# Two 4 KB half buffers per block of expert weights, or one 8 KB buffer

## The chip, the cores and the metric

One core of one Trainium2 chip runs the whole kernel in one launch. The metric is the device time of a launch in microseconds (us); the kernel before took 1304.69 us (median of 3 runs, 1304.62 to 1304.88).

## The reference

A trunk of two layers over 256 tokens of width 1024, all in float32. Each layer has a mixer (three groups of heads that read one input projection, and one output projection) and then a mixture of 32 SwiGLU experts; each is followed by a residual and a layer norm. Cut to what matters here:

```
for i in range(DEPTH):                       # 2
    mix = hybrid_mixer(h, w_in[i], ..., w_out[i])
    h = layer_norm(ALPHA * h + mix)
    ffn = hierarchical_moe(h, ..., w_gate[i], w_up[i], w_down[i])
    h = layer_norm(ALPHA * h + ffn)
# one expert e:  (silu(xb @ w_gate[e]) * (xb @ w_up[e])) @ w_down[e]
# w_gate, w_up: (2, 32, 1024, 512), w_down: (2, 32, 512, 1024), float32
```

Every expert's weights are read once in each layer: 2 x 32 x 6 MB, 402.7 million bytes.

## The kernel before

**Experts.** A layer's experts are taken four at a time, in eight quarters (`for q in range(NE // QE)` in `moe`). The weights come in blocks of 1 MB: `blocks(l)` cuts each gate and up matrix into two blocks of 512 rows and each down matrix into two of 256 rows. The order is: first halves of four gates, second halves of four gates, the same for up, the same for down; 24 blocks a quarter, 192 a layer. In memory a block is 128 rows of 8 KB, one for each partition of the on-chip buffer. TensorE works on four blocks together (a group): `up` runs k outside and the four experts inside, so that a group starts in earnest when the last of its four blocks is there, and the four buffers are read to the end of the group. With `k` it goes through a block's four pieces of 512 columns in their order, so that the first 4 KB of each row are done with in the middle of a group.

**Buffers.** `load_rows(src, kind)` loads a block. Kind "R" takes one 8 KB buffer of the ring `w` (5 of them, `wslot`) with one DMA. Kind "H" takes two 4 KB buffers of the ring `wh` (10 of them, `whalf`) with a DMA of 512 KB each. In the steady part R and H alternate, so that of each group two blocks are R and two are H. Kind "X" is an 8 KB buffer of another ring (`wwide`), and a string such as "rrrr" is four 2 KB buffers (`wq`). The first 21 blocks of a layer have kinds written out by hand (`KINDS`, five of them H); they are issued while the mixer still runs, as buffers come free. The last five blocks before the final four of layer 1 are all H (`tail`), so that the R ring is free for the next layer's input weights. The last four blocks of a layer are loaded in 256 KB pieces (`load_last`, L1448). All of this goes through the queue of SyncE (SP) in one order; an issue that waits holds up those behind it.

**Split weights.** In the mixers the ring `wh` has another use: `split` makes of a weight piece a rounded high part (ScalarE, L404, listed under the helper's line L148) and the low rest (VectorE or GpSimd, L412), each in a 4 KB buffer, and `mm3` multiplies the parts in three matmuls for each k (L419, L420, L421). In the input projections L419 and L420 read the high part and L421 the low one. `ahead` keeps up to three splits ready.

Of the kernel before, what the change touches and what calls it, by code (L numbers as in the profile page):

```python
# [9 lines left out]
F32 = mybir.dt.float32  # L10
# [6 lines left out]
L, T, D = 2, 256, 1024  # L17
# [3 lines left out]
QE = 4  # L21
NR = 5
NX = 3
NH = 10
PB = dict(r=3, d=3, s=2)
WB = dict(x=1, r=27, d=9, s=7, sh=4)
PRI = ("r", "side", "s", "g", "d")
# [60 lines left out]
def hybrid_trunk(ctx, tc, x, w_in, w_sm, pp, sw, rows, w_r, lnv, cst, w_out,  # L88
# [3 lines left out]
    ring = ctx.enter_context(tc.tile_pool(name="ring", bufs=NR))  # L92
    hring = ctx.enter_context(tc.tile_pool(name="hring", bufs=NH))
    wk = ctx.enter_context(tc.tile_pool(name="wk", bufs=1))
# [3 lines left out]
    def shaped(t, shape):  # L98
        n = 1
        for s in shape:  # L100
            n *= s
        v = t[:, 0:n]
        if len(shape) == 2:
            v = v.rearrange("p (a b) -> p a b", a=shape[0])
        elif len(shape) == 3:
            v = v.rearrange("p (a b c) -> p a b c", a=shape[0], b=shape[1])
        elif len(shape) == 4:
            v = v.rearrange("p (a b c d) -> p a b c d", a=shape[0], b=shape[1], c=shape[2])
        return v
# [8 lines left out]
    def w512(*shape, name="w", tag=None):  # L118
        t = tag or cur[0]
        return shaped(wk.tile([128, 512], F32, tag="w_" + t, name=name, bufs=WB[t]), shape)  # L120
# [5 lines left out]
    def wide(name):  # L126
        return ring.tile([128, 2048], F32, tag="xs", name=name, bufs=NX)

    def quarters_of(v):
        return [[v[:, (2 * t + n) * 512:(2 * t + n + 1) * 512] for n in range(2)] for t in range(2)]  # L130
# [16 lines left out]
    def act(out, in_, func, **kw):  # L147
        i = nc.scalar.activation(out, in_, func, **kw)  # L148
        if func in tabs:
            chain_t(i)  # L150
        return i
# [4 lines left out]
    def after(a, b):  # L156

        tc.add_manual_dep(a.ins, b.ins.name, mybir.DependencyInfo(mybir.DependencyClass.NoSync,
                                                                  mybir.DependencyReason.DATA), reason="order")
# [234 lines left out]
    def slot():  # L394
        return ring.tile([128, 2048], F32, tag="w", name="wslot")
# [4 lines left out]
    def split(w, eng=None):  # L400

        n = w.shape[1:]
        hi = shaped(hring.tile([128, 1024], F32, tag="wh", name="whi"), n)
        i = act(hi.bitcast(F32R), w, AF.Copy)  # L404
        if last[0] is not None:
            after(i, last[0])
        last[0] = i
        nsub[0] += 1
        if eng is None:
            eng = G if nsub[0] % SUBV == 0 and nsub[0] > SV else V  # L410
        lo = shaped(hring.tile([128, 1024], F32, tag="wh", name="wlo"), n)
        i = eng.tensor_tensor(out=lo.bitcast(F32R), in0=w, in1=hi, op=OP.subtract)  # L412
        if eng is V and normed[0] is not None:
            after(i, normed[0])
        return hi.bitcast(F32R), lo.bitcast(F32R)
# [24 lines left out]
    def fetch(out, in_):  # L440

        i = nc.sync.dma_start(out=out, in_=in_)
        if order[0]:
            if order[0] is not True:
                after(i, order[0])
            order[0] = i

    def load_rows(src, kind):

        k, n = src.shape[0] // 128, src.shape[1]  # L450
        src = src.rearrange("(p k) c -> p (k c)", p=128)
        if kind in "RX":
            v = slot() if kind == "R" else wide("wwide")
            fetch(v, src)
            return [v[:, j * 512:(j + 1) * 512] for j in range(4)]
        if kind == "H":
            r = []
            for i in range(2):
                v = hring.tile([128, 1024], F32, tag="wh", name="whalf")
                fetch(v, src[:, i * 1024:(i + 1) * 1024])  # L460
                r += [v[:, 0:512], v[:, 512:1024]]
            return r
        r = []
        for j in range(4):
            v = w512(512, name="wq", tag=kind[j])
            fetch(v, src[:, j * 512:(j + 1) * 512])
            r.append(v)
        return r


    class Weights:
# [15 lines left out]
        def ahead(self, n, eng=None):  # L487

            while self.order and len(self.wp) < n:
                n_, m = self.order.pop(0)  # L490
                w = self.w[n_]
                self.wp[n_, m] = split(w[:, m] if isinstance(n_, int) else w[:, m * 4:(m + 1) * 4] if n_ == "gv"
                                       else w[:, :, m * 128:(m + 1) * 128], eng)
# [735 lines left out]
    def moe(l, src, part, early, WR, RT):  # L1229
# [79 lines left out]
        def residual(t, n):  # L1309

            p = ps(4, 128, tag="r" if t * 2 + n < RS0 else "s")
            for k in range(4):
                if 2 * t + n < RS0:
                    PE.transpose(p[:, k], h[t][n][:, k * 128:(k + 1) * 128], ident)
                    continue
                for a in range(2):
                    mm(p[:, k], lhsT=zp[a][t][n][:, k * 128:(k + 1) * 128], rhs=IDR.bitcast(F32R), start=(a == 0), stop=(a == 1))
            e = w512(4, 128, name="res", tag="s")
            for k in range(4):
                (A if 2 * t + n < RS0 else nc.scalar).activation(e[:, k], p[:, k], AF.Identity, scale=DP[:, l, 25 + 4 * n + k:26 + 4 * n + k],  # L1320
                    bias=DP[:, l, 33 + 4 * n + k:34 + 4 * n + k])
            yield
            for k in range(4):
                (PE.matmul if 2 * t + n < RS0 else mm)(acc[t][n][:, k * 128:(k + 1) * 128], lhsT=e[:, k], rhs=ident,
                                                       start=(k == 0 and 2 * t + n < RS0), stop=False)
# [93 lines left out]
        iota = c("iota", CAP)[:, None, :].to_broadcast([128, 2 * QE, CAP])  # L1419
        srcs = iter(blocks(l)[len(early):])  # L1420
        nb = 6 * NE - len(early) - QE
        tail = ["H"] * (NH // 2) if l + 1 < L else []
        kinds = iter(((["R", "H"] * nb)[:nb - len(tail)]) + tail)

        for i in range(ISSUE, len(early)):
            early[i] = load_rows(*early[i])
        order[0] = None

        def take():
            return early.pop(0) if early else load_rows(next(srcs), next(kinds))  # L1430
# [108 lines left out]
        for q in range(NE // QE):  # L1539
# [8 lines left out]
            r = residual(*divmod(q - RES + RS0, 2)) if 0 <= q - RES < 4 - RS0 else iter(())  # L1548
# [80 lines left out]
    src, h, gi, W = xin, xin, 0, Weights(0)  # L1629
# [5 lines left out]
    for l in range(L):  # L1635
        xT = transposed(src, h, p_(l, "gx", 0, 8), p_(l, "bx", 0, 8), between)
        if l == 0:
            setup()
        last[0] = last_x[LX]
        WR = w512(8, 36, name="WR", tag="x")  # L1640
        nc.sync.dma_start(out=WR, in_=w_r[l].rearrange("(k p) c -> p k c", p=128))
        F, part, RT = mixer(l, h, xT, gi, W, WR)
        if stages == "mixer":
            break
        early, order[0] = list(zip(blocks(l), KINDS)), True
        for i in range(ISSUE):
            early[i] = load_rows(*early[i])
        acc, zp, RM, GA, cnti = moe(l, F, part, early, WR, RT)
        overflow(l, zp, acc, RM, GA, cnti)
        if l + 1 < L:  # L1650
            W = Weights(l + 1)
            src, h, gi = acc, quarters_of(wide("h")), 4 + 4 * l
# [85 lines left out]
```

## Time and profile before

| | before |
|---|---|
| median of 3 runs | 1304.69 us |
| the profiled execution, its own time | 1305.92 us |
| its span in the trace | 1304.1 us |
| TensorE busy | 1038.0 us, 80% of the span |
| VectorE, ScalarE, GpSimd busy | 29%, 19%, 10% |
| read from memory | 440.82 MB |
| DMA packets | 127917, of them 104656 under 8 KB |

The span is the time from the first to the last instruction in the trace; the profiled execution's own time has 1.8 us around it. The busy shares are means over stages: two mixers (about 0 to 205 us and 650 to 845 us), and two stretches of experts behind them.

### The profile page before, as it was taken

Reading aid. Unit: us, or ns where it says so; the run is one execution under the profiler, and the core shown is the slowest. Engines: PE = TensorE matmul, PEld = TensorE weight load, DVE = VectorE, ACT = ScalarE, POOL = GpSimd, SP = SyncE. Lnnn points to the kernel's source line nnn. Section 1 sums busy time; section 2 is a strip of 40 time slices with the busy share of each in tenths; the row PEclk is TensorE's granted clock in tenths of the full one; section 3 lists DMA queues with packets and bytes.
Section 4 is the critical chain, followed back from the end, with each engine's and each line's share of the span. In section 5 each row is a group of like instructions: output and inputs, shape, how many; then the busy total and the mean of one; then the engine's idle time right before and its main releaser. Section 6 shows DMA issues by size and latency. Waiting matters only on the chain. (4 is left out here: it accounts for less than half of the span.)

```text
span 1304.1 us, 18012 instructions
## 1 busy us (share of the span) xinstructions
PE 1038.0 (80%) x7412; PEld 530.9 (41%) x7412; DVE 378.2 (29%) x842; ACT 252.1 (19%) x442; POOL 129.4 (10%) x121
## 2 busy tenths in 40 slices
PE   6899989787768677777788999896977777776765
PEld 5788783242123113211177887632411321131211
DVE  5888861020001000100269787510100110010002
ACT  4535532010000000000154453310100000010100
POOL 4234110000000000000033440100000000000001
PEclk9899989898998898898988999899889899889988
DMA  9343688999999999999973357699999999999995
GB/s 303 115 123 139 249 305 320 415 414 416 415 415 415 415 416 414 416 415 414 338 237 100 122 190 249 249 398 416 415 415 415 415 415 415 415 415 414 415 415 195
DMA packets 127917, 443.18 MB, mean 340 GB/s; under 512 B 16848, under 2 KB 41808, under 8 KB 104656
## 3 DMA queue, kind: packets, MB, share of 16 engines
q1 hardware_dynamic: 126256, 439.28, 86.3%
q10 hardware_dynamic: 1440, 2.62, 0.6%
q8 instruction: 62, 1.02, 0.3%
q14 instruction: 31, 0.25, 0.1%
q0 software_dynamic: 128, 0.01, 0.0%
HBM read 440.82 MB, written 1.05 MB: 339 GB/s over the span
## 5 line engine op out<-in xcount | busy, mean ns | idle before, releaser
L1489 PE MATMUL ps<-wslot,xg 128*32 128x512 f32 x968 | 323.1, 711 | 125.0 <-DMA wslot<-in_w_up_dram 88.1
L1489 PE MATMUL ps<-whalf,xg 128*32 128x512 f32 x984 | 317.7, 707 | 9.3 <-DMA whalf<-in_w_up_dram 7.9
L1489 PEld LDWEIGHTS ps<-wslot,xg 128*32 128x32 f32 x968 | 70.8, 126 | 345.4 <-issue 152.7
L1525 PE MATMUL ps<-wslot,hT 128*32 128x512 f32 x432 | 145.8, 631 | 26.8 <-DMA wslot<-in_w_down_dram 26.7
L1495 DVE TENSOR_TENSOR hh<-ps,hh 128x256 f32<-128x256 f32 x32 | 12.1, 419 | 495.6 <-PE ps L1489 429.6
L1525 PE MATMUL ps<-whalf,hT 128*32 128x512 f32 x448 | 148.1, 626 | 1.1 <-DMA whalf<-in_w_down_dram 1.1
L419 PE MATMUL ps<-xh,whi 128*128 128x256 f32 x320 | 95.7, 300 | 0.7 <-issue 0.7
L421 PE MATMUL ps<-xh,wlo 128*128 128x256 f32 x320 | 92.6, 290 | 2.7 <-DVE wlo L412 2.7
L420 PE MATMUL ps<-xl,whi 128*128 128x256 f32 x320 | 93.1, 292 | 0.0
L1489 PEld LDWEIGHTS ps<-whalf,xg 128*32 128x32 f32 x984 | 66.8, 125 | 56.4 <-DMA whalf<-in_w_up_dram 34.8
L1531 DVE SCALAR_TENSOR_TENSOR yy<-ps,gs,yy 128x512 fp32r<-128x512 f32 x32 | 24.0, 751 | 224.7 <-ACT yy L148 220.8
L412 POOL TENSOR_TENSOR wlo<-wslot,whi 128x1024 fp32r<-128x1024 f32 x26 | 63.3, 2436 | 143.5 <-ACT whi L148 113.3
L148 ACT ACTIVATE whi<-wslot 128x1024 fp32r<-128x1024 f32 x62 | 64.5, 1054 | 62.5 <-PE ps L420 48.7
L148 ACT ACTIVATE hT<-ps 128x256 f32<-128x256 f32 x32 | 12.3, 384 | 316.6 <-PE ps L1511 316.6
L1469 PE MATMUL ps<-oh,z 128*128 128x256 f32 x256 | 66.1, 418 | 7.8 <-DVE gs L1505 4.0
L1525 PEld LDWEIGHTS ps<-wslot,hT 128*32 128x32 f32 x432 | 30.9, 112 | 96.5 <-issue 50.0
L1469 PEld LDWEIGHTS ps<-oh,z 128*128 128x128 f32 x256 | 61.8, 329 | 16.2 <-issue 7.8
L148 ACT ACTIVATE yy<-ps,gs 128x512 fp32r<-128x512 f32 x32 | 22.0, 687 | 226.4 <-PE ps L1525 192.8
L421 PEld LDWEIGHTS ps<-xh,wlo 128*128 128x128 f32 x320 | 62.6, 196 | 4.1 <-DVE wlo L412 2.9
L419 PEld LDWEIGHTS ps<-xh,whi 128*128 128x128 f32 x320 | 62.6, 196 | 3.7 <-issue 2.0
L1534 PE MATMUL ps<-yy,gT 128*128 128x512 f32 x128 | 46.9, 447 | 21.3 <-ACT yy L148 16.0
L420 PEld LDWEIGHTS ps<-xl,whi 128*128 128x128 f32 x320 | 62.8, 197 | 2.0 <-issue 1.9
(386 smaller groups left out, 1251.5 us busy)
## 6 DMA issues: line engine op xcount, KB each, us to landing
whalf<-in_w_up_dram SPq DMA_DIRECT2D x134, 512.0 KB, 12.6
wslot<-in_w_gate_dram SPq DMA_DIRECT2D x62, 1024.0 KB, 13.8
wslot<-in_w_up_dram SPq DMA_DIRECT2D x59, 1024.0 KB, 13.8
whalf<-in_w_down_dram SPq DMA_DIRECT2D x112, 512.0 KB, 12.9
whalf<-in_w_gate_dram SPq DMA_DIRECT2D x112, 512.0 KB, 12.8
wslot<-in_w_down_dram SPq DMA_DIRECT2D x54, 1024.0 KB, 13.8
wslot<-in_w_in_dram SPq DMA_DIRECT2D x22, 1024.0 KB, 7.3
wq<-in_w_down_dram SPq DMA_DIRECT2D x64, 256.0 KB, 7.0
```

The costliest lines, as they stand in the source:

```text
L148: i = nc.scalar.activation(out, in_, func, **kw)
L412: i = eng.tensor_tensor(out=lo.bitcast(F32R), in0=w, in1=hi, op=OP.subtract)
L419: return (mm(out, lhsT=lhs[0], rhs=rhs[0], start=start, stop=False), mm(out, lhsT=lhs[0], rhs=rhs[1], start=False, stop=False), mm(out, lh ...
L420: mm(out, lhsT=lhs[0], rhs=rhs[1], start=False, stop=False),
L421: mm(out, lhsT=lhs[1], rhs=rhs[0], start=False, stop=stop))
L1469: mm(p[:, i, :], lhsT=zp[a][t][k // 4][:, k % 4:512:4], rhs=oh[:, t].rearrange("p a b -> p (a b)"), start=(t + a == 0), stop=(t + a == 2))
L1489: mm(pp_[es], lhsT=xg[k // 2][:, k % 2, o + es.start:o + es.stop], rhs=Wx[j][k // 4][k % 4], start=(k == 0), stop=(k == 7))
L1495: V.tensor_tensor(out=hh[:, w], in0=pu[:, w], in1=hh[:, w], op=OP.mult)
L1525: mm(py[n][es], lhsT=hT[:, k, es], rhs=Wd[j][k // 2][k % 2 * 2 + n], start=(k == 0), stop=(k == 3))
L1531: V.scalar_tensor_tensor(yl.bitcast(F32R), py[n], gs, yh, op0=OP.mult, op1=OP.subtract)
L1534: mm(acc[t][n], lhsT=gT[:, t * 128:(t + 1) * 128], rhs=v.bitcast(F32R), start=(q + k == 0 and 2 * t + n >= RS0), stop=(q + k == NE // QE))
```

## The change

`split` takes one 8 KB buffer for both parts; kind "H" loads a whole block into one 8 KB buffer with one 1 MB DMA, as R and X do; the ring `wh` has 5 buffers of 8 KB in place of 10 of 4 KB, and the tail counts them as they are. The order of the blocks and their kinds stays.

```diff
-NH = 10
+NH = 5
@@ split
         n = w.shape[1:]
-        hi = shaped(hring.tile([128, 1024], F32, tag="wh", name="whi"), n)
+        v = hring.tile([128, 2048], F32, tag="wh", name="wparts")
+        hi, lo = shaped(v, n), shaped(v[:, 1024:2048], n)
         i = act(hi.bitcast(F32R), w, AF.Copy)
...
-        lo = shaped(hring.tile([128, 1024], F32, tag="wh", name="wlo"), n)
         i = eng.tensor_tensor(out=lo.bitcast(F32R), in0=w, in1=hi, op=OP.subtract)
@@ load_rows
-        if kind in "RX":
-            v = slot() if kind == "R" else wide("wwide")
+        if kind in "RXH":
+            v = slot() if kind == "R" else wide("wwide") if kind == "X" else hring.tile([128, 2048], F32, tag="wh", name="wring")
             fetch(v, src)
             return [v[:, j * 512:(j + 1) * 512] for j in range(4)]
-        if kind == "H":
-            r = []
-            for i in range(2):
-                v = hring.tile([128, 1024], F32, tag="wh", name="whalf")
-                fetch(v, src[:, i * 1024:(i + 1) * 1024])
-                r += [v[:, 0:512], v[:, 512:1024]]
-            return r
@@ moe
-        tail = ["H"] * (NH // 2) if l + 1 < L else []
+        tail = ["H"] * NH if l + 1 < L else []
```

## Rows read from the trace of the kernel before

**Rows 1.** The page, 40 slices of the span: DMA busy share and rate.

```profile
DMA  9343688999999999999973357699999999999995
GB/s 303 115 123 139 249 305 320 415 414 416 415 415 415 415 416 414 416 415 414 338 237 100 122 190 249 249 398 416 415 415 415 415 415 415 415 415 414 415 415 195
```

**Rows 2.** Windows: engines' busy us (instructions), TensorE's granted clock, DMA share, GB/s.

```profile
260.00:600.00 340.00, 257.63 (x1296) 85.05 (x1288) 27.09 (x72) 23.04 (x45) 0.00 (x0) 0.91 1.02 415
...
612.00:624.00 12.00, 9.57 (x56) 2.31 (x57) 0.00 (x0) 0.00 (x0) 0.00 (x0) 0.86 1.02 410
...
777.50:783.50 6.00, 5.80 (x90) 4.39 (x86) 6.00 (x18) 4.13 (x11) 1.23 (x2) 1.00 1.00 420
...
862.00:1270.00 408.00, 303.51 (x1562) 100.42 (x1555) 29.52 (x79) 29.29 (x57) 2.18 (x4) 0.92 1.02 415
```

**Rows 3.** Waits of SP's queue, 230 to 600 us: us in total, times, longest.

```profile
SPq L442 <- DMA wslot<-in_w_up_dram: 50.1, 24, 2.2
...
SPq L442 <- DMA whalf<-in_w_gate_dram: 34.8, 40, 0.9
SPq L442 <- PE ps L1489: 25.7, 26, 6.4
```

**Rows 4.** DMA packets of the alternating stretch, 320 to 560 us.

```profile
DMA packets 20469, 99.60 MB, mean 415 GB/s; under 512 B 2271, under 2 KB 2271, under 8 KB 14369
```

**Rows 5.** DMA packets of the end of layer 1, 612 to 624 us.

```profile
DMA packets 1216, 4.92 MB, mean 410 GB/s; under 512 B 134, under 2 KB 134, under 8 KB 1096
```

**Rows 6.** DMA packets in the second mixer, 777.5 to 783.5 us.

```profile
DMA packets 346, 2.52 MB, mean 420 GB/s; under 512 B 36, under 2 KB 36, under 8 KB 39
```

**Rows 7.** The page, DMA issues: count, KB each, median us to landing.

```profile
whalf<-in_w_up_dram SPq DMA_DIRECT2D x134, 512.0 KB, 12.6
wslot<-in_w_gate_dram SPq DMA_DIRECT2D x62, 1024.0 KB, 13.8
...
whalf<-in_w_down_dram SPq DMA_DIRECT2D x112, 512.0 KB, 12.9
whalf<-in_w_gate_dram SPq DMA_DIRECT2D x112, 512.0 KB, 12.8
```

**Rows 8.** Timeline of SP's queue, early H loads of layer 1.

```profile
161.34 6.51 SPq L442 DMA_DIRECT2D whalf<-in_w_up_dram  x4
...
168.43 7.33 SPq L442 DMA_DIRECT2D whalf<-in_w_up_dram  x6
```

**Rows 9.** Timeline of SP's queue, 284 to 306 us.

```profile
289.73 0.33 SPq L442 DMA_DIRECT2D wslot<-in_w_up_dram  x1
297.30 0.80 SPq L442 DMA_DIRECT2D whalf<-in_w_up_dram  x2
300.27 0.33 SPq L442 DMA_DIRECT2D wslot<-in_w_up_dram  x1
```

**Rows 10.** Tile `wslot`, 112 to 125 us: two 1 MB loads on an idle queue.

```profile
DMA to landing us min/median/max: 4.8/4.8/4.9
```

**Rows 11.** Tile `whalf`, 230 to 600 us.

```profile
DMA to landing us min/median/max: 7.6/12.7/14.4
```

**Rows 12.** Tile `whalf`, 600 to 640 us, the tail of layer 1.

```profile
DMA to landing us min/median/max: 6.5/10.7/13.8
```

**Rows 13.** Waits, all engines: us in total, times, longest.

```profile
ACT whi L148 <- PE ps L420: 48.7, 25, 6.3
```

**Rows 14.** Timeline of TensorE in the first mixer.

```profile
23.37 0.28 PE L420 MATMUL ps<-xl,whi 128*128 128x256 f32 x1
23.49 0.28 PE L421 MATMUL ps<-xh,wlo 128*128 128x256 f32 x1
```

**Rows 15.** Timeline of ScalarE, 8 to 20 us.

```profile
13.60 0.63 ACT L148 ACTIVATE xh<-xT 128x512 fp32r<-128x512 f32 x1 [0.16 <-DVE xT L317]
```

**Rows 16.** Timeline of GpSimd, 8 to 22 us.

```profile
13.15 2.68 POOL L326 TENSOR_TENSOR xl<-xT,xh 128x512 fp32r<-128x512 f32 x2
```

## The prediction

> **What bounds the kernel now.** I looked first at the slices of the page [rows 1]. In two long runs of slices, twelve and fourteen of them, the DMA digit is 9 and the rate stands at 414 to 416 GB/s with nothing in between. These are the expert stretches. The windows say the same with the other engines beside it: from 260 to 600 us and from 862 to 1270 us the DMA share is 1.02 at 415 GB/s, while TensorE is busy for 257.63 of 340 us and 303.51 of 408 us, 76% and 74% [rows 2]. (A share above 1 means that the packets of an engine overlap a little.) So these stretches end when the bytes are in, and TensorE waits for blocks. The two mixers are the opposite: DMA digits of 3 to 7, buffers full. A change in the loads is therefore worth what it does to the rate of the expert stretches, and little elsewhere.
>
> Then SP's own waits. From 230 to 600 us its queue is held mostly by the landing of earlier DMAs (six rows, of 50.1 us down to 34.8 us), and only 25.7 us, 26 times, by a matmul that still reads the buffer to be filled [rows 3]. SP issues as far ahead as it may: an R load lands 13.8 us after its issue [rows 7], but 4.8 us on an idle queue [rows 10]. About 9 us of transfers usually stand ahead of a new one; that cushion hides any issue that comes a few us late.
>
> Last, what the rate depends on. The packets of a stretch are counted by size; a packet under 512 B goes with the end of a DMA on one of the 16 engines. In the alternating stretch 14369 - 2271 = 12098 packets are of 4 KB and about 6100 of 8 KB: an H row comes as two packets, an R row as one [rows 4]. That is 415 GB/s. At the end of layer 1, where H blocks follow one another, 962 of 1216 packets (3.94 of 4.92 MB) are of 4 KB: 410 GB/s [rows 2, 5]. In the second mixer three whole blocks follow one another for 6 us, with 307 packets of 8 KB and 3 smaller ones of data: 420 GB/s at a DMA share of 1.00 [rows 2, 6]. The three are in the order of the packet size.
>
> **The steady H loads.** Each becomes one DMA of 8 KB rows like R. A block is 1.0486 MB. At 420 GB/s it takes 2.497 us. In the alternating stretch a block takes 2.527 us at 415 GB/s, the mean of R and H; with R at 2.497 us an H block takes 2.557 us. The change saves 0.060 us for each H block that passes while the DMA engines are the bound. The page counts 134 + 112 + 112 = 358 halves, 179 blocks [rows 7]; ten of them are early loads, five a layer, in the mixers where the DMA engines have idle time (4 + 6 halves in layer 1, the same in layer 2) [rows 8]. So 169 x 0.060 = 10.1 us.
>
> Bounds: 420 is read over only 6 us, where one or two packets of 8 KB more or less at the edges are 1.4 to 2.7 GB/s; I allow 2. 415 is firm to 0.5. With 418 to 422 GB/s the saving per H block is 0.036 to 0.084 us, so 6.1 to 14.2 us. The end of layer 1 gives a check: 80% of its bytes are halves at 2.557 us a block on the whole, which puts a half pair at 2.572 us, a saving of 0.075 us; it lies within. I take 0.060, from the longer row.
>
> The Trainium skill (DMA: Bandwidth & Descriptors, "Why small descriptors are slow (HBM only)") speaks against so much: it puts the fixed cost at about 3 cycles a packet on beats of 32 bytes and calls joining worth it only up to 256 B. By that, two 4 KB packets are 262 cycles and one of 8 KB 259, an estimate of 1.1% of an H block or 4.9 us in all. The difference of 415 and 420 GB/s in the rows above is twice that; the smaller gain is a rival below.
>
> **The later release.** Before, the first half of an H buffer is free in the middle of a group; after, only at its end, like an R buffer. Behind a waiting H load stand all later loads of the queue, and TensorE waits for those. The tightest place that I found is at 297.30 us: two halves go out after a long wait, and the next R load, which needs a buffer that the group reads to its end, follows at 300.27 us [rows 9]. A whole H load would go at about 300.27 us instead, 3.0 us later, and could land 4.8 us behind it on an idle queue [rows 10], at 305.1 us. The load before it went at 289.73 us and lands some 13.8 us later [rows 7], at 303.5 us, so that an unbroken stream would bring the next whole block at 306.0 us. The cover is 0.9 us. Elsewhere it is larger: 7.6 us is the shortest way to landing of any half from 230 to 600 us against a median of 12.7 us [rows 11]; in the tail of layer 1 the shortest is 6.5 us [rows 12], 1.7 us above the idle queue. If the cover goes, the price is what the issue is late, up to 3.0 us a place. I take 1.0 us in all for a few short gaps; bounds 0 and 8 x 2.1 = 17 us (3.0 less 0.9 at each of the eight pairs of quarters with a gather, the largest work that delays a group).
>
> **The mixers.** Before, ScalarE waits 25 times for L420, the last reader of a high part, to write the next one there [rows 13]. Now it must wait for L421 too, which starts 0.12 us later [rows 14]: at most 25 x 0.12 = 3.0 us on ScalarE. The splits are made up to three ahead, so the wait ends long before its product is needed; I take 0. The first products of a layer read the high part before the low one exists. If the two parts of one buffer were watched as one, they would wait. The buffer of `xh` shows that parts are watched apart: GpSimd reads one quarter of it at 13.15 us while ScalarE still writes another at 13.60 us [rows 15, 16]. So 0 here too. The ten early H loads save five issues a layer in a time when the DMA engines are partly idle, and the first-half buffer's earlier release there is worth the same 0.12 us: 0.
>
> **Sum.** -10.1 + 1.0 = -9.1 us. The profiled execution's span of 1304.1 us becomes 1295.0 us, its own time of 1305.92 us becomes 1296.8 us. The median of the runs shown is 1.2 us below that own time, so I forecast 1295.6 us.
>
> **The rivals.**
>
> A smaller gain. The fixed part of a packet is smaller than the 6 us window says, and whole blocks stream at 417 GB/s. Then an H block saves 2 x 0.0125 = 0.024 us, 169 of them 4.1 us, and with 1.0 us of gaps the time is 1301.6 us. For it speaks the shortness of that window, against it the 410 GB/s of the tail, which lie as far on the other side.
>
> No gain. Something behind the DMA engines holds the stream at about 415 GB/s whatever the packets are: 1304.7 us, with the gaps 1305.7. Against it: 420 GB/s in one window. The same page of the Trainium skill (section "Where 436 GB/s comes from") has two ceilings, 435 GB/s on the side of SBUF and some 358 for a core's share of HBM; the 415 GB/s here are above the second, so only the first can bind, and it leaves room for 420.
>
> Slower. The whole buffers come back too late, and the queue runs dry where a gather holds up TensorE, at eight places by 2.1 us each (above): 16.8 us lost against 10.1 gained, 1311.4 us. It decides against the change from 10.1 / 16 = 0.63 us of dry queue a quarter. For it speaks the small cover at 297.30 us; against it that the R loads have lived with the same late release all along at a share of 1.02, and a deeper cushion elsewhere: 13.8 us to landing [rows 7], at three DMAs every 2 x 2.527 us, are about eight DMAs under way (an estimate), and eight whole ones hold more.
>
> That the change does not do what it says is excluded: R blocks of the same rows come as 8 KB packets now.
>
> That TensorE becomes the bound is excluded too: it is busy 76% and would be 77% at a rate 1.2% higher.
>
> **How the numbers follow.** The forecast (6 to 14 us saved, less small gaps) has 0.66, the smaller gain (2.6 to 6 us) 0.17, no gain to be told 0.09, slower 0.08. A measurement of this kernel can tell about 0.2%, 2.6 us, from no change: faster 0.83, same 0.09, slower 0.08. The range goes from the largest saving without gaps, 1304.7 - 14.2 = 1290.5 us, to the smaller gain's 1301.6 us.
>
> **What would show it.** Right: the rate of the expert slices rises from 415 to 418 to 422 GB/s at the same share; packets fall by 144 for each of 179 blocks, to about 102100, and those under 8 KB to about 56000; SP waits more for L1489 and less for landings; both expert stretches shorten by about 5 us, the mixers by nothing. Wrong: slices below 415 GB/s or with an 8 among the 9s at the quarters (gaps), a rate of 415 to 416 (no gain), or ScalarE's wait on L421 with TensorE waiting for `wparts` in the mixers.

## The result, and the profile after

The changed kernel takes 1340.65 us (median of 4 runs, 1339.88 to 1349.43), the kernel before 1304.79 us beside it (4 runs). The ratio is 1.0289, 95% interval 1.0252 to 1.0326: 2.9% slower. The forecast was 9.1 us less; it became 36 us more. The profiled execution took 1339.88 us, with a span of 1338.1 us in place of 1304.1 us.

The slices of the page, against [rows 1]:

```profile
DMA  9343688999997999899973356699899989989995
GB/s 305 104 150 113 234 297 336 421 400 421 421 422 298 422 420 421 331 421 422 334 236 96 120 198 223 255 403 421 369 422 421 407 332 420 421 337 413 421 420 220
```

Two things are to be seen. Between the dips the rate is 420 to 422 GB/s where it was 414 to 416: the stream itself is faster, as forecast. But six slices fall to 400, 298, 331, 369, 332 and 337 GB/s, three in each stretch of experts, one for every second quarter (407 and 413 beside two of them belong to the same dips). In windows (columns as in [rows 2]), first two undisturbed ones and then one around each dip:

```profile
300.00:400.00 100.00, 75.16 (x362) 21.75 (x362) 4.03 (x9) 5.01 (x10) 0.00 (x0) 0.95 1.01 421
895.00:945.00 50.00, 38.28 (x183) 15.60 (x186) 3.76 (x10) 3.29 (x7) 0.00 (x0) 0.91 1.01 421
262.00:300.00 38.00, 34.89 (x169) 17.38 (x169) 7.16 (x22) 5.46 (x12) 0.00 (x0) 1.00 0.97 402
400.00:430.00 30.00, 26.48 (x126) 10.27 (x125) 5.14 (x16) 2.40 (x4) 0.00 (x0) 0.83 0.69 282
530.00:575.00 45.00, 34.91 (x177) 10.44 (x176) 3.49 (x12) 2.99 (x5) 0.00 (x0) 0.85 0.86 354
945.00:975.00 30.00, 26.63 (x158) 10.26 (x151) 3.40 (x12) 3.37 (x7) 0.00 (x0) 0.96 0.88 363
1065.00:1090.00 25.00, 22.53 (x123) 9.29 (x122) 4.91 (x16) 2.39 (x4) 0.00 (x0) 0.93 0.70 281
1195.00:1225.00 30.00, 24.16 (x134) 7.16 (x136) 3.49 (x12) 2.39 (x4) 2.18 (x4) 0.86 0.78 318
```

A window of width w at a rate r has lost w x (1 - r / 421): 1.7, 9.9, 7.2, 4.1, 8.3 and 7.3 us, 38.5 us of dry queue in all. The stages bear this out (us). Mixer 1 ends with the first gather matmul, experts 1 and 2 with the last matmul of the combine; mixer 2 is taken to the first gate matmul, 7.7 us behind the first gather matmul of its layer.

| | mixer 1 | experts 1 | mixer 2 | experts 2 | end | span |
|---|---|---|---|---|---|---|
| before | 188.7 | 459.5 | 191.5 | 452.0 | 12.4 | 1304.1 |
| after | 193.1 | 474.8 | 193.6 | 464.1 | 12.5 | 1338.1 |

The experts are 15.3 and 12.1 us longer, 27.4 us: 38.5 us lost and some 11 us saved. The mixers add 4.4 and 2.1 us.

**What SP waits for.** The waits of its queue from 230 to 600 us, against [rows 3]:

```profile
SPq L442 <- PE ps L1482: 148.8, 30, 10.5
SPq L442 <- PE ps L1518: 76.1, 16, 21.4
SPq L442 <- remote: 23.8, 1, 23.8
SPq L442 <- DMA wring<-in_w_up_dram: 21.2, 12, 2.1
```

(Lines from there on are 7 lower than before: L1482 is the gate and up matmul, L1518 the down matmul, L1462 the gather matmul.) SP now waits for TensorE to be done with a buffer, once, at the third gather, for 21.4 us. The longest wait, 23.8 us, is at the second gather; "remote" says that the profile can't name what ended it, and the timelines below show what SP waited for. The timeline of SP there:

```profile
389.20 0.38 SPq L442 DMA_DIRECT2D wslot<-in_w_gate_dram  x1
414.50 0.33 SPq L442 DMA_DIRECT2D wring<-in_w_gate_dram  x1
```

For 25.3 us nothing is issued. The load of 389.20 us lands at 408.1 us by its record. The next, issued at 414.50 us, lands at 419.2 us, 4.7 us later, as on an idle queue [rows 10]; an unbroken stream would have it 2.5 us behind its forerunner, at 410.6 us: 8.6 us of dry queue. So work already in the queue covers 16.7 us of a pause. What TensorE does meanwhile:

```profile
390.69 1.90 PE L1518 MATMUL ps<-wring,hT 128*32 128x512 f32 x4
392.53 0.98 PE L1462 MATMUL ps<-oh,z 128*128 128x256 f32 x3
393.43 1.90 PE L1518 MATMUL ps<-wslot,hT 128*32 128x512 f32 x4
395.27 1.91 PE L1462 MATMUL ps<-oh,z 128*128 128x256 f32 x7
397.80 2.61 PE L1462 MATMUL ps<-oh,z 128*128 128x256 f32 x10 [0.63 <-DVE xg L1471]
400.34 3.42 PE L1518 MATMUL ps<-wring,hT 128*32 128x512 f32 x4
403.69 1.21 PE L1462 MATMUL ps<-oh,z 128*128 128x256 f32 x4
406.02 0.44 PE L1491 MATMUL ps<-C,oh 128*128 128x128 f32 x2 [1.11 <-ACT xg L148]
406.29 0.51 PE L1493 MATMUL ps<-GA,oh 128*128 128x4 f32 x4
407.97 0.66 PE L1491 MATMUL ps<-C,oh 128*128 128x128 f32 x2 [1.17 <-DVE gs L1498]
408.42 0.85 PE L1493 MATMUL ps<-GA,oh 128*128 128x4 f32 x4
409.21 1.06 PE L1518 MATMUL ps<-wslot,hT 128*32 128x512 f32 x1
```

A down matmul (L1518) shows as two records, so "x4" is a pair. The down matmuls free the buffers that SP waits for: eight loads go out from 414.50 to 420.50 us. Six down matmuls run in three pairs with the gather between, the third pair in 3.42 us in place of 1.90, because the granted clock is 0.50 then (window in the last section); then come transposes and gate matmuls of the next two quarters (L1491, L1493), which wait 1.11 us for ScalarE and 1.17 us for VectorE. Only at 409.21 us, 18.5 us after the first, does the bulk of the down matmuls start. The same place in the kernel before (timeline of TensorE):

```profile
385.05 0.62 PE L1525 MATMUL ps<-whalf,hT 128*32 128x512 f32 x1
...
387.53 2.61 PE L1469 MATMUL ps<-oh,z 128*128 128x256 f32 x10
390.76 3.67 PE L1469 MATMUL ps<-oh,z 128*128 128x256 f32 x14 [0.62 <-DVE xg L1478]
394.36 1.01 PE L1525 MATMUL ps<-wslot,hT 128*32 128x512 f32 x1
```

Here the gather is in one piece, no transpose stands before the down matmuls, and they go on at 394.36 us, 9.3 us after the first of them at 385.05 us. The order of an engine's instructions is not in the source: both sources have the gather, the matmuls and the transposes in the same order, and the build's scheduler interleaves them. Read from the two traces, at the second and the third gather of a layer (h transposes of the product, D down matmul, G gather matmul, t and g transposes and gate matmuls of the next two quarters, C combine):

```
before: h4 D6 G24 D12 t2 g2 t2 g2 D11 C4 D3
after:  h4 D2 G3 D2 G17 D2 G4 t2 g2 t2 g2 D23 C2 D3
```

The first gather of a layer has the same parting, but no transposes ahead of the down matmuls; its dips are the two smallest, 1.7 and 4.1 us.

So the theory from these traces (B below): the whole loads are faster, and what costs is another order of TensorE's work around the gathers, which the build chose when the loads had another size. The rival (A below) is the one forecast as "Slower": whole buffers come back too late, whatever the order.

### The profile page after: what moved, and what is told of

Same layout as the page of the kernel before. It is cut to its first block, busy times and chain, and to the rows that moved or that the text cites. A ratio compares the mean times of both kernels' runs of the same rounds, so it can differ in the third digit from the quotient of the medians.

```text
span 1338.1 us, 17733 instructions
## 1 busy us (share of the span) xinstructions
PE 1085.4 (81%) x7412; PEld 542.9 (41%) x7412; DVE 383.4 (29%) x842; ACT 251.7 (19%) x442; POOL 129.6 (10%) x121
## 2 busy tenths in 40 slices
DMA packets 102139, 443.16 MB, mean 331 GB/s; under 512 B 13984, under 2 KB 38944, under 8 KB 55968
## 5 line engine op out<-in xcount | busy, mean ns | idle before, releaser
L1482 PE MATMUL ps<-wslot,xg 128*32 128x512 f32 x968 | 316.4, 688 | 84.9 <-DMA wslot<-in_w_up_dram 55.9
L1482 PE MATMUL ps<-wring,xg 128*32 128x512 f32 x984 | 313.9, 692 | 58.8 <-DMA wring<-in_w_up_dram 42.6
L1482 PEld LDWEIGHTS ps<-wslot,xg 128*32 128x32 f32 x968 | 69.9, 123 | 295.7 <-issue 135.3
L1518 PE MATMUL ps<-wring,hT 128*32 128x512 f32 x448 | 162.8, 648 | 5.1 <-DMA wring<-in_w_down_dram 5.0
L1488 DVE TENSOR_TENSOR hh<-ps,hh 128x256 f32<-128x256 f32 x32 | 12.1, 420 | 509.3 <-PE ps L1482 444.1
L1518 PE MATMUL ps<-wslot,hT 128*32 128x512 f32 x432 | 146.0, 643 | 9.5 <-DMA wslot<-in_w_down_dram 9.5
L1482 PEld LDWEIGHTS ps<-wring,xg 128*32 128x32 f32 x984 | 64.6, 123 | 120.2 <-DMA wring<-in_w_up_dram 71.1
L419 PE MATMUL ps<-xh,wparts 128*128 128x256 f32 x320 | 96.7, 303 | 0.1
L421 PE MATMUL ps<-xh,wparts 128*128 128x256 f32 x320 | 92.9, 291 | 2.9 <-DVE wparts L412 2.9
L420 PE MATMUL ps<-xl,wparts 128*128 128x256 f32 x320 | 91.9, 288 | 0.0
L412 POOL TENSOR_TENSOR wparts<-wslot,wparts 128x1024 fp32r<-128x1024 f32 x26 | 64.4, 2476 | 154.6 <-ACT wparts L148 125.8
L1462 PEld LDWEIGHTS ps<-oh,z 128*128 128x128 f32 x256 | 62.4, 328 | 25.0 <-issue 14.9
L148 ACT ACTIVATE hT<-ps 128x256 f32<-128x256 f32 x32 | 12.3, 383 | 317.8 <-PE ps L1504 317.8
L1462 PE MATMUL ps<-oh,z 128*128 128x256 f32 x256 | 68.1, 414 | 4.1 <-DVE xg L1471 3.7
L148 ACT ACTIVATE wparts<-wslot 128x1024 fp32r<-128x1024 f32 x62 | 64.3, 1050 | 29.9 <-PE ps L421 22.9
L1518 PEld LDWEIGHTS ps<-wslot,hT 128*32 128x32 f32 x432 | 31.3, 115 | 84.6 <-issue 56.3
L421 PEld LDWEIGHTS ps<-xh,wparts 128*128 128x128 f32 x320 | 62.6, 196 | 4.5 <-DVE wparts L412 3.3
L419 PEld LDWEIGHTS ps<-xh,wparts 128*128 128x128 f32 x320 | 62.8, 197 | 3.7 <-issue 1.9
L420 PEld LDWEIGHTS ps<-xl,wparts 128*128 128x128 f32 x320 | 62.7, 196 | 1.2 <-issue 1.1
## 6 DMA issues: line engine op xcount, KB each, us to landing
wring<-in_w_up_dram SPq DMA_DIRECT2D x67, 1024.0 KB, 14.5
wring<-in_w_gate_dram SPq DMA_DIRECT2D x56, 1024.0 KB, 14.5
```

Source lines behind the costliest of these rows:

```text
L419: return (mm(out, lhsT=lhs[0], rhs=rhs[0], start=start, stop=False), mm(out, lhsT=lhs[0], rhs=rhs[1], start=False, stop=False), mm(out, lh ...
L420: mm(out, lhsT=lhs[0], rhs=rhs[1], start=False, stop=False),
L421: mm(out, lhsT=lhs[1], rhs=rhs[0], start=False, stop=stop))
L1462: mm(p[:, i, :], lhsT=zp[a][t][k // 4][:, k % 4:512:4], rhs=oh[:, t].rearrange("p a b -> p (a b)"), start=(t + a == 0), stop=(t + a == 2))
L1482: mm(pp_[es], lhsT=xg[k // 2][:, k % 2, o + es.start:o + es.stop], rhs=Wx[j][k // 4][k % 4], start=(k == 0), stop=(k == 7))
L1488: V.tensor_tensor(out=hh[:, w], in0=pu[:, w], in1=hh[:, w], op=OP.mult)
```

## The experiments

All ratios are to the kernel before, run beside them on the same chip (1306.36 us for e1 to e4, 1306.39 for e5 and e6, 1307.48 for e7 to e9, 1306.80 for e10 and e11).

**e1: whole buffers, halves loaded.** The changed kernel, with an H block's 1 MB fetched by two DMAs into its one buffer.

```diff
-            fetch(v, src)
+            for i in range(2 if kind == "H" else 1):
+                fetch(v[:, i * 1024:(i + 1) * 1024] if kind == "H" else v, src[:, i * 1024:(i + 1) * 1024] if kind == "H" else src)
```

> The changed kernel with its 8 KB buffers, but each H block is loaded by two DMAs of 512 KB into the two halves of its buffer; TensorE's order of gather and down matmuls is then that of the kernel before. Theory A (the late give-back of a whole buffer runs the queue dry): about 1330 to 1350 us, rate of the expert slices with dips as in the changed kernel. Theory B (the 1 MB loads led to another order of TensorE's matmuls around the gathers, and that order gives the buffers back late): 1300 to 1312 us, rate flat at 415 GB/s.

Measured: 1312.98 us (1308.94 to 1315.51), ratio 1.0041 (1.0019 to 1.0064). In both stretches of experts TensorE's order is that of the kernel before, matmul for matmul; in the mixers it differs from it, and is that of the changed kernel. The rates of the page:

```profile
GB/s 302 114 149 111 236 314 312 415 414 413 415 416 414 416 415 416 415 415 407 317 235 98 122 198 203 253 396 415 414 407 415 415 415 415 414 415 415 416 415 198
```

413 to 416 GB/s, but for two slices of 407, one at the end of layer 1's experts and one at the first gather of layer 2, where 0.8 us are lost. The buffers are whole here and come back at the end of a group: SP waits 45.0 and 31.8 us for gate and up and for down matmuls from 230 to 600 us, against 25.7 and 15.3 us before, though never longer than 8.6 us. So the later release by itself does not dry the queue, with loads of 512 KB: the rival falls for them, and e5 tries it with 1 MB. The time is 1 us above theory B's range. The profiled execution's span (1313.2 us) is 9 us longer than the one before; 5 us of that are mixers (190.7 and 194.8 us), the rest experts (462.7 and 452.6 us).

**e2 and e3: the down matmuls in one chain.** Each down matmul must follow the one before, in the order half of k, output half, k, expert; e2 on the changed kernel, e3 on the kernel before.

```diff
-            for i in range(2 if last else 1):
+            prev = None
+            for i in range(2):
...
-                            mm(py[n][es], lhsT=hT[:, k, es], ...)
+                            m = mm(py[n][es], lhsT=hT[:, k, es], ...)
+                            if prev is not None and not last:
+                                after(m, prev)
+                            prev = m
```

> The changed kernel with the down matmuls of a quarter (but the last) held in one order: first half blocks, output half 0 then 1, k, and the four experts innermost, so that four neighbours use four different column groups. Loads of 1 MB and 8 KB buffers as in the changed kernel. Theory B (order): the dips at every second quarter vanish or shrink to under 3 us each, slices at 420 to 422 GB/s, 1290 to 1308 us (what the mixers lost, 6.5 us, may stay). Theory A (late give-back): the dips stay, 1325 us or more.

> The kernel before with the same held order of the down matmuls: the control for the run above. Both theories: 1298 to 1310 us at 415 GB/s.

Measured: e2 1323.76 us (1320.06 to 1328.97), ratio 1.0116 (1.0089 to 1.0143); e3 1317.32 us (1311.95 to 1321.38), ratio 1.0071 (1.0042 to 1.01). Both expectations are missed, e2 between its two theories and e3 above its range. The gather's matmuls were not part of the chain, and the scheduler put them between single down matmuls (D16 G4 D1 G10 D1 G10 t2 g2 D1 t2 g2 D6 ... in e2). So this was a bad order too: it costs with either size of load, more with the whole ones.

**e4: pairs alone.** The kernel before, with the first six down matmuls held in pairs of both output halves of one expert, the gather still in one piece (D6 G24).

```diff
+                    todo = ([(n, a, j) for j in range(3) for n in range(2)] + [(0, a, 3)] + [(0, a + 1, j) for j in range(4)]
+                            + [(1, a, 3)] + [(1, a + 1, j) for j in range(4)])
+                for n, k, j in todo:
...
+                    if prev is not None and not last:
+                        after(m, prev)
```

> The kernel before, with 4 KB half buffers and 512 KB loads, but the down matmuls held in the order that the changed kernel has: both output halves of one expert after each other, so that neighbours use the same column group. Theory B (order): slower than before by 5 to 35 us, with dips at the quarters that have a gather. Theory A (late give-back): within 4 us of before.

Measured: 1306.24 us (1303.62 to 1309.2), ratio 0.9998 (0.9986 to 1.001). Theory B's expectation is missed and theory A's met; but the run does not have the changed kernel's order, since the gather was not parted. Pairs cost nothing when the gather is not parted and the loads are halves.

**e5 and e6: a good order held by hand.** Six down matmuls, then three quarters of the next gather (24 matmuls), then the other 26 down matmuls, then the rest of the gather; e5 on the changed kernel, e6 on the kernel before.

```diff
-        def gather(q):
+        def gather(q, prev=None, part=(0, 1, 2, 3)):
...
+                    todo = [(0, a, 0), (0, a, 1), (1, a, 0), (0, a, 2), (1, a, 1), (1, a, 2), (0, a, 3)]
+                    todo += [(0, a + 1, j) for j in range(4)] + [(1, a, 3)] + [(1, a + 1, j) for j in range(4)]
+                for c_, (n, k, j) in enumerate(todo):
+                    if c_ == 6 and i == 0 and q % 2 and not last:
+                        prev = gather(q + 1, prev, (0, 1, 2))
...
+            if q % 2 and not last:
+                gather(q + 1, prev, (3,))
```

> The changed kernel (8 KB buffers, 1 MB loads) with TensorE's order around the gathers held as the kernel before had it: six down matmuls, the first three quarters of the next gather, the other 26 down matmuls in half-block order, then the last quarter of the gather. Theory B (the order set by the 1 MB loads gives the buffers back late): no dip of over 2 us at the quarters, slices at 420 to 422 GB/s, both expert stretches shorter than in the kernel before (under 459 and 452 us), 1290 to 1304 us. Theory C (with 1 MB loads and whole buffers the queue runs dry whatever the order): dips stay, 1315 us or more.

> The kernel before (4 KB halves, 512 KB loads) with the same held order: the control. 1300 to 1310 us, 415 GB/s without dips in all theories.

Measured: e5 1296.73 us (1295.98 to 1301.11), ratio 0.9928 (0.9905 to 0.9951); e6 1304.68 us (1302.87 to 1309.13), ratio 0.9981 (0.9966 to 0.9997). With the same order around the gathers on both sides, the change is worth 8.0 us, to some 4 us either way. (It is not quite the order of the kernel before: the gather's other 8 matmuls, a quarter ahead there, stand behind the down matmuls here, and the transposes too. e6 alone is some 2 us faster than the kernel before.) The windows of e5, SP at the second gather, TensorE there, and SP's waits from 230 to 600 us:

```profile
260.00:600.00 340.00, 264.98 (x1320) 89.31 (x1316) 26.89 (x72) 23.45 (x45) 0.00 (x0) 0.90 1.01 421
...
862.00:1270.00 408.00, 314.20 (x1593) 104.33 (x1583) 30.09 (x81) 30.08 (x58) 2.18 (x4) 0.92 1.01 421
```

```profile
385.70 0.38 SPq L442 DMA_DIRECT2D wslot<-in_w_gate_dram  x1
397.99 0.33 SPq L442 DMA_DIRECT2D wring<-in_w_gate_dram  x1
```

```profile
387.52 0.62 PE L1533 MATMUL ps<-wring,hT 128*32 128x512 f32 x1
...
389.37 5.88 PE L1466 MATMUL ps<-oh,z 128*128 128x256 f32 x24
395.18 0.62 PE L1533 MATMUL ps<-wslot,hT 128*32 128x512 f32 x1
```

```profile
SPq L442 <- PE ps L1490: 165.3, 35, 8.1
SPq L442 <- PE ps L1533: 76.9, 13, 11.7
```

421 GB/s over 340 and 408 us with no dip; SP's pause is 12.3 us in place of 25.3, and the bulk of the down matmuls starts 7.7 us after the first. In sum SP waits as much for TensorE as in the changed kernel (L1490 and L1533 are its L1482 and L1518); what differs is the longest wait. So theory C, and with it the rival, falls for loads of 1 MB too.

**e7, e8 and e9: the changed kernel's order, rebuilt.** e7 holds the kernel before to D2 G3 D2 G17 D2 G4 t2 g2 t2 g2 D26 at the second and third gather of each layer; e8 holds the changed kernel to the same; e9 is e8 with the transposes behind the down matmuls (D2 G3 D2 G17 D2 G4 D26 G8).

```diff
+                    if c_ in (2, 4, 6) and i == 0 and q % 2 and not last:
+                        if c_ == 2:
+                            steps = gather(q + 1, (0, 1, 2))
+                        prev = advance(steps, prev, {2: 3, 4: 17, 6: 4}[c_])
+                        if c_ == 6 and q > 1:
+                            for r_ in (q + 1, q + 2):
+                                ready[r_], prev = pgts(r_, prev)
...
```

The last three lines hold the transposes and gate matmuls ahead of the other down matmuls; e9 leaves them out.

> The kernel before (4 KB halves, 512 KB loads) with TensorE held in the order that the changed kernel had at its second and third gather of a layer: two down matmuls of one expert, 3 gather matmuls, two, 17, two, 4, then the transposes and gate matmuls of the next two quarters, and only then the other 26 down matmuls. Theory B (that order alone is what gives the buffers back late): dips at the gathers and 1315 to 1340 us. Theory D (the order costs that only where a block is given back whole): 1303 to 1311 us, 415 GB/s.

> The changed kernel (8 KB buffers, 1 MB loads) with the same held order: the control. Both theories: 1320 to 1342 us, with dips of 5 to 9 us at the second and third gather of a layer, as in the changed kernel.

> The changed kernel with the gather parted by pairs of down matmuls as above, but the transposes of the next quarters behind the down matmuls. If the transposes with their waits for VectorE are the larger half of the delay: 1296 to 1306 us with dips under 3 us. If the parted gather is: 1312 us or more.

Measured: e7 1314.08 us (1309.6 to 1322.47), ratio 1.0065 (1.004 to 1.0089); e8 1319.79 us (1314.74 to 1322.2), ratio 1.0117 (1.0082 to 1.0151); e9 1300.65 us (1299.5 to 1303.57), ratio 0.996 (0.9941 to 0.9978). e7 lies between its two theories, with dips of up to 3.9 us; e8 is just under its range, with dips of 3.2 to 6.0 us where 5 to 9 were expected; e9 is inside its own. By the medians the order costs the halves 9.4 us (e7 less e6) and the whole loads 23.1 us (e8 less e5); 19.1 us of the latter are the transposes and their waits ahead of the down matmuls (e8 less e9), 3.9 us the parting of the gather (e9 less e5; the kernel before differed by 1.1 us between these two chips). The intervals leave each of these some 4 to 5 us either way, so the last is barely told from nothing. So the same order costs more than twice as much where a block is given back whole. But e8 is not the whole loss: the changed kernel is 21 us slower still.

**e10 and e11: only the transposes moved.** e10 is the changed kernel with the transposes held behind the last down matmul of the quarter before; the rest of TensorE's order around the gathers stays the scheduler's (D2 G3 D2 G17 D2 G4 D23 C2 D3 t2 ...). e11 is e5 again on this chip.

```diff
-                nc.tensor.transpose(pgt[:, t * 128:(t + 1) * 128], ohp[t], ident)
+                m = nc.tensor.transpose(pgt[:, t * 128:(t + 1) * 128], ohp[t], ident)
+                if downed[0] is not None:
+                    after(m, downed[0])
...
-                            mm(py[n][es], lhsT=hT[:, k, es],
+                            downed[0] = mm(py[n][es], lhsT=hT[:, k, es],
```

> The changed kernel with one thing more: the two transposes of a quarter's one-hot matrix (and with them the two gate matmuls) must follow the last down matmul of the quarter before. TensorE's order of the other instructions stays as it was in the changed kernel: two down matmuls, 3 of the gather, 2 down, 17, 2 down, 4, then now the other down matmuls. If the transposes with their waits for VectorE, ahead of the down matmuls, hold the buffers back, most of the dry queue goes: dips of a microsecond or two at the six gathers in place of 2 to 10, rates of 410 to 421 GB/s in all slices of the experts, and 1302 to 1312 us in place of 1340.7. Rival: the parting of the gather with pairs on one column group is what costs, or something in the changed kernel that the orders written out by hand did not copy; then the dips stay at 5 us or more and the time at 1320 us or above.

> The kernel with the order held and whole buffers once more, unchanged, beside the other on the same chip: 1295 to 1299 us, 0.5 to 0.9% below the kernel before. If its gain was a matter of one chip, it is within 0.3% of the kernel before.

Measured: e11 1299.19 us (1295.89 to 1300.16), ratio 0.9926 (0.9904 to 0.9949): the gain of e5 again. e10 1319.2 us (1312.49 to 1324.6), ratio 1.0097 (1.0067 to 1.0126). Its expectation is missed: 21 us of the 36 us loss against the kernel before go with this one edge (1340.65 less 1319.2), but the time lies between the two theories, just under the rival's, and the dips, 1.6 to 3.2 us, too. The timeline of e10 at the same place shows what is left:

```profile
387.60 1.90 PE L1521 MATMUL ps<-wring,hT 128*32 128x512 f32 x4
...
394.71 2.61 PE L1463 MATMUL ps<-oh,z 128*128 128x256 f32 x10 [0.63 <-DVE xg L1472]
397.25 3.50 PE L1521 MATMUL ps<-wring,hT 128*32 128x512 f32 x4
400.68 1.21 PE L1463 MATMUL ps<-oh,z 128*128 128x256 f32 x4
401.82 0.62 PE L1521 MATMUL ps<-wslot,hT 128*32 128x512 f32 x1
```

The wait of 0.63 us for `xg` and the third pair at 3.50 us in place of 1.90 us are still there; from 397.4 to 400.8 us, while that pair runs, the granted clock is 0.50. In e9 neither is, and the granted clock is 1.00 from the first down matmul on: there the gather's other 8 matmuls come behind the down matmuls, not a quarter ahead as in e10 and in the changed kernel. Five kernels with whole loads stand in one row when they are sorted by SP's longest pause at the second gather of layer 1 (from the start of the last issue before it to the next, from the timelines). The dry queue is the sum over all six gathers, each in a window of 53 us from 8 us before it, by the same rule as above:

| | SP's pause | first down matmul to the bulk | dry queue | median | the profiled execution |
|---|---|---|---|---|---|
| e5 | 12.3 us | 7.7 us | 0.1 us | 1296.73 us | 1301.11 us |
| e9 | 16.4 us | 11.7 us | 3.9 us | 1300.65 us | 1300.87 us |
| e10 | 18.5 us | 14.2 us | 14.5 us | 1319.20 us | 1312.49 us |
| e8 | 21.2 us | 15.1 us | 17.7 us | 1319.79 us | 1314.74 us |
| after | 25.3 us | 18.5 us | 38.6 us | 1340.65 us | 1339.88 us |

Up to some 16 us the queue covers the pause; beyond it the time is paid at up to six gathers. (The profiled executions of e8 and e10 lie at the low end of their times, so their pauses are if anything those of a good execution.)

## Why the prediction was wrong

**The steady H loads: right.** Packets fell to 102139, those under 8 KB to 55968, as forecast to the hundred. The rate rose to 421 GB/s, inside 418 to 422. The saving was given as 10.1 us (6.1 to 14.2): e5 against e6, the same order on both sides, has experts of 457.4 and 445.0 us against 461.0 and 452.9 us, 11.5 us less (profiled executions, in both the slowest of the kernel's runs). The number of DMAs fell with the packets, and no run parts the two. The fixed cost of a packet in the Trainium skill (DMA: Bandwidth & Descriptors, "Why small descriptors are slow (HBM only)"), by which the gain would have been 4.9 us, an estimate, is too small for this stream: these stretches show more than twice as much. (In [rows 1] the second run of slices at 414 to 416 GB/s has twelve, not fourteen; nothing hangs on it.)

**The later release: the step that failed.** It stood in the sum with 1.0 us, with bounds of 0 and 17 us, and 38.5 us were measured. Its mechanism was named rightly (a late buffer, behind it all later loads, a gather that holds TensorE up), and so were SP's new waits and the dips at the quarters as a sign of it. What failed is its unspoken premise, that TensorE would do its work around a gather in the order of the trace before. The lateness of 3.0 us a place was read off that order. The new program has another one, in which the bulk of the down matmuls starts 18.5 us after the first instead of 9.3 us, and a dip costs 1.7 to 9.9 us, at six places, not 2.1 us at eight. That the later release is nearly harmless in the old order was right: e1 has it and loses 1.1 us at all six gathers.

**The rival "Slower"** got 0.08. Its place and its sign came true, its reason only in part: with the old order it does not happen, and with the new one, as rebuilt in e7 and e8, whole blocks lose 23.1 us where halves lose 9.4. The argument against it, that R loads had lived with the same late release all along, rested on the same premise.

**The range** ended at 1301.6 us and missed by 39 us. With the order held by hand, e5 and e11 have 1296.73 and 1299.19 us, near the forecast of 1295.6 us. The nearness is in part luck: some 2 us are the held order's own (e6), and the mixers take back part of what the experts gain.

**The mixers: taken as 0, too little.** The second mixer takes 193.6 to 195.5 us in all eight profiled kernels with whole buffers (after, e1, e2, e5, e8 to e11) and 189.4 to 191.8 us in all five with halves; e5 loses 3.7 us there against e6. The first mixer does not part them: 190.0 to 193.1 us with whole buffers, 188.7 to 191.9 us with halves, so the 4.4 us there are not explained. ScalarE's new wait for L421 is not longer than the old one for L420 (22.9 us against 48.7 us in [rows 13]). What differs is ScalarE's order, in the second mixer of after and of before:

```profile
793.92 0.60 ACT L148 ACTIVATE gate<-ps 128x512 f32<-128x512 f32 x1 [1.34 <-PE ps L421]
794.53 1.28 ACT L154 ACT_TABLE_LOAD   x1
795.83 1.06 ACT L148 ACTIVATE wparts<-wslot 128x1024 fp32r<-128x1024 f32 x1
```

```profile
774.50 1.06 ACT L148 ACTIVATE whi<-wslot 128x1024 fp32r<-128x1024 f32 x1 [0.87 <-ACT gate L148]
775.47 0.58 ACT L148 ACTIVATE gate<-ps 128x512 f32<-128x512 f32 x1
776.07 1.28 ACT L154 ACT_TABLE_LOAD   x1
```

The high part is written behind `gate` and the table load instead of ahead of them, so GpSimd's low part comes later and falls beside an operation of VectorE (GpSimd and VectorE of after, then VectorE of before):

```profile
796.96 2.36 POOL L412 TENSOR_TENSOR wparts<-wslot,wparts 128x1024 fp32r<-128x1024 f32 x1 [5.86 <-ACT wparts L148]
```

```profile
797.31 2.16 DVE L1061 TENSOR_SCALAR KB<-cum,rb 128x256 f32<-128x256 f32 x1
```

```profile
777.86 0.35 DVE L1068 TENSOR_SCALAR KB<-cum,rb 128x256 f32<-128x256 f32 x1
```

VectorE's operation takes 2.16 us in place of 0.35 us and ends within 0.2 us of GpSimd's. All eight kernels with whole buffers have one such operation in each mixer, and none of the five with halves has any. This is read from traces only; no run moved that one instruction, and TensorE's order in the mixers differs too. As e1 has it all with loads of 512 KB, it comes with the whole buffers and not with the 1 MB loads.

**What stays open.** Why the build chose the other order is argued, not shown: e1 shows that two loads of 512 KB in place of one of 1 MB, with nothing else changed, bring the old order back in the experts, so the loads' form decides there; that the scheduler reckons with a time for each load is a likely way. And e8 copies the changed kernel's order at two of the three gathers of a layer, with the gather's other 8 matmuls behind the down matmuls and not a quarter ahead; 21 us lie between it and the changed kernel, as much as between their dry queues (38.6 and 17.7 us). The waits of 0.63 and 1.11 us and the third pair at the slow clock, which e8 has not, fit that, but no run gives them back one by one.

## What to carry to other kernels

Where a build orders an engine's instructions, an edit of a DMA's size can change the order of matmuls that it does not touch; so compare the program order of each engine before the difference in time is put down to the edit, and where a queue lives on buffers that come back in time, hold the order around the longest job by hand. The number to watch is the longest time in which the loading queue issues nothing against what it has under way: here, with whole loads, a pause of 12 us was free and one of 25 us cost 10 us. With the order held, the changed kernel beats the kernel before (e5, ratio 0.9928).

## What the runs showed of the hardware

- One stream of 8 KB rows into this core runs at 421 GB/s for hundreds of microseconds (windows of e5), against 415 GB/s with half of the rows in two packets of 4 KB (windows of [rows 2]).
- Down matmuls of four different experts, which use 32 columns of TensorE each, run side by side: in e10 one takes 0.62 us and four start together at 401.82 us, the next at 402.27 us. Four records of one expert go one after the other: 1.90 us (387.60 us), in which time sixteen of the former start.
- The third pair of down matmuls in the changed kernel, and after the waits at 406 and 408 us the bulk of them, ran at a granted clock of 0.50, that is 1.2 GHz (1.06 us a record in the bulk, windows below); in e5, where TensorE had no wait there, the bulk ran at 1.00, 2.4 GHz, and 0.62 us. From the start of the bulk to SP's next issue it is 2.8 us at all eighteen gathers of e5, e9 and e10, and 4.0 to 5.4 us at five of the six gathers of the changed kernel and at the four of e8 that have the transposes ahead, all with a granted clock of 0.50 in it. So a part of the longest pauses is the clock. The slow clock and the waits were seen together and not varied apart; if they belong together, a wait is paid a second time in the work behind it.

The windows of after (TensorE alone), and that of e5 (all engines):

```profile
400.60:404.00 3.40, 3.40 (x5) 0.50 1.01 419
409.30:414.00 4.70, 4.70 (x24) 0.50 0.00 0
```

```profile
395.20:398.80 3.60, 3.60 (x33) 1.02 (x32) 1.00 (x2) 0.00 (x0) 0.00 (x0) 1.00 1.02 421
```

- VectorE's operation of 0.35 us beside a GpSimd operation of 2.36 us took 2.16 us, and both ended within 0.2 us (rows above). This fits the Trainium skill (SBUF — State Buffer, "SBUF: two separate sides"): the two engines share a pair of ports, VectorE uses it in a 2-port mode or with two inputs in SBUF, and the one that comes first holds it for its whole instruction. The trace does not show which ports this operation used.
